# Hybrid decoder layer on one core: norm factors of three query projections moved into the exponentials, the first norm's row and the rotation tables moved later

## The chip, the cores and the metric

The kernel runs on one NeuronCore of a Trainium2 chip. The time of a run is the device time of that core in microseconds (us). The engines named below are TensorE (PE in the rows; its weight loads PEld), VectorE (DVE), ScalarE (ACT), GpSimd (POOL) and SyncE (SP), which here only issues DMAs. TensorE's clock has two levels, 1.2 and 2.4 GHz; a granted clock of 1.00 in a row is the higher one, 0.50 the lower.

## The reference

One decoder layer over 256 tokens of width 1024, all in float32. Cut to what matters here:

```python
hn = rmsnorm(h, mix_norm_g)                       # first norm
conv_a, conv_b, q, k_c, v_c, k_s, v_s, k_w, v_w, gate_logits = split(hn @ w_in)
y_conv = silu(layernorm(depthwise_conv31(conv_a * sigmoid(conv_b)) + b_dw))
y_nsa  = nsa_mixer(...)        # three softmax attentions on q: compressed keys (q as it is),
                               # selected blocks and window (q, k rotated by partial_rope(positions))
h = h + concat(y_conv, y_nsa) @ w_out
hq = rmsnorm(h, mem_q_norm_g)                     # second norm
h = h + memory_attention(hq, rmsnorm(mem, mem_kv_norm_g), ...)   # softmax(q k^T / 16) v @ w_o
hp = rmsnorm(h, peer_norm_g)                      # third norm
s  = (hp @ peer_w_q) . sub_keys                   # 8 heads x 2 sides x 128 scores per token
# top 16 of each side, top 16 of the 256 sums, gates = softmax over these 16
h = h + sum over experts of gates * gelu(hp . u_e) * v_e
return rmsnorm(h, final_norm_g)

def rmsnorm(x, g): return x * rsqrt(mean(x * x, -1) + 1e-6) * g
```

An RMS norm multiplies each token's vector by one number, 1/rms, after the gain. A projection is linear, so this number can be applied to the product instead. In a softmax over scores of one token the positive number can be applied as late as in the exponential: exp(r * (s - max s)).

## The kernel before

Activations lie transposed: 128 features on the partitions, the 256 tokens along the row. A projection takes the raw activations times the gain (hx for the first norm, g1 for the second, gx for the third) and makes one output chunk of 128 features by 256 tokens in PSUM. The first projection (`proj1`, L160) uses plain float32: 8 products, 16 matmul records of 128x256 per chunk. The later ones (`proj`, L156) split each operand into a high and a low part and take three products (24 matmuls per chunk); `wsplit` (L134) makes the parts of each 128x1024 weight chunk with two ScalarE copies (hi) and two subtractions (lo) on VectorE, or on GpSimd for the first 34 expert chunks. Weight chunks of 512 KB are loaded through SP's queue into four buffers `raw`.

The norm factor is made by the class `Rstd` (L197). `add` squares one chunk on ScalarE and adds it up on VectorE. `sums` (L214) takes the column sums with two tiny matmuls (ss), makes 1/rms on VectorE with twelve dependent instructions on 128x2 (m, sh, rsc, t) and two diagonal matrices dg. `rows` (L229) turns that into a 128x256 tile with the factor of every token along the row: two products with `ones` (sr), one ScalarE copy. `col` is the factor with tokens on the partitions, `row` the one with tokens along the row. The first norm (tag x) makes its row in the middle of chunk pa1, the second (tag h1) behind the third query chunk of the memory attention (L765 to L772), the third (tag h2) behind the third of 16 expert-query chunks (L846 to L861). (The rows print h1 and h2 without their numbers, as sr_h and dg_h.)

The stages in order: 14 warm-up matmuls; four pairs pb, pa of convolution chunks; two chunks kv; six chunks pq (two of keys, four of queries) with `rope` (L374: a permutation matmul rp, two multiplies with the tables Ct and St and an add on VectorE); the chunk group pv in natural layout; then 16 attention units of scores, softmax and transposes, interleaved by hand with the memory keys and values as filler matmuls (`fill`); w_out; the memory attention's queries (`mq_chunk`, `mq_out`, `m_scores`); w_mem_o; expert queries (`pq_out`, `key_scores`); then 128 expert chunks u and 128 v with the expert choice on VectorE behind the first.

The depthwise convolution is 124 VectorE instructions on yc (31 taps for 4 chunks, `tap`), handed out a few at a time by `conv(n)`; the rest must be done at unit 12, where `ln_mean` adds up the four chunks and TensorE's matmul pmu (L616) takes the mean over the channels.

TensorE's order is the program's. The order on VectorE, ScalarE, GpSimd and SP is made by a planner when the kernel is built: it takes the earliest instruction in program order that is ready by its own estimate of times, so it also takes later ones early into gaps. At run time each engine's queue is fixed and in order. PSUM has two tags of four slots: "mm" for projections, "at" for small and attention tiles.

The rotation tables: L250 and L251 load the positions to all 128 partitions (each reads the same 1 KB) between the first weight chunk and the rest of x; L263 to L279 make the angles on VectorE with two columns (`inv`, `sgn`) of the parameter tile `par`; L333 to L335 make St and Ct with ScalarE's Sin and load the Tanh table again.

Of the kernel before, what the change touches and what calls it, by code (L numbers as in the profile page):

```python
# [20 lines left out]
P = 128  # L21
T = 256
# [12 lines left out]
for _name, _w in (("mix_g", 8), ("memq_g", 8), ("memkv_g", 8), ("peer_g", 8), ("conv_w", 4 * TAPS),  # L35
                  ("conv_b", 4), ("ln_g", 4), ("ln_b", 4), ("cmp_b1", 2), ("cmp_b2k", 1),
                  ("cmp_b2v", 64), ("cmp_pos", 32), ("inv", 1), ("sgn", 1)):
    PC[_name] = (_n, _n + _w)
    _n += _w
# [12 lines left out]
def constants():  # L52
# [37 lines left out]
def rope_constants():  # L90

    d = np.arange(P) % 64
    inv = (np.float32(500000.0) ** (-(np.arange(8, dtype=np.float32) * np.float32(2.0) / np.float32(16.0)))).astype(np.float32)
    return np.stack([np.where(d < 16, inv[d % 8], 0.0), np.where(d < 8, -1.0, np.where(d < 16, 1.0, 0.0))], axis=1).astype(np.float32)


def build(tc, A, out, dbg=None):
# [99 lines left out]
    class Rstd:  # L197
# [16 lines left out]
        def sums(self):  # L214
# [9 lines left out]
            rsqrt(y, m, t, sh)  # L224
            self.diag = mwk.tile([P, 2, P], F32, name=f"dg_{self.tag}", tag="rs_d", bufs=1)
# [24 lines left out]
    posi = wk.tile([P, T], I32, name="posi", tag="rt")  # L250
    nc.sync.dma_start(posi, A["pos"].partition_broadcast(P))  # L251
# [9 lines left out]


    posf = wk.tile([P, T], F32, name="posf", tag="tb")  # L263
    V.tensor_copy(posf, posi)
    ang = St = ch.tile([P, T], F32, name="St")
    V.tensor_scalar(ang, posf, Pm("inv"), None, op0=ALU.mult)
    kk = wk.tile([P, T], F32, name="kk", tag="ta")
    MAGIC = 12582912.0
    V.tensor_scalar(kk, ang, 1.0 / (2.0 * math.pi), MAGIC, op0=ALU.mult, op1=ALU.add)
    V.tensor_scalar(kk, kk, MAGIC, None, op0=ALU.subtract)  # L270
    c1 = 6.28125
    c2 = float((np.array([2.0 * math.pi - c1], np.float32).view(np.uint32) & np.uint32(0xFFFFF000)).view(np.float32)[0])
    c3 = 2.0 * math.pi - c1 - c2
    for c in (c1, c2, c3):
        V.scalar_tensor_tensor(ang, kk, -c, ang, op0=ALU.mult, op1=ALU.add)
    PIF = 3.1415925
    V.tensor_scalar(ang, ang, PIF, -PIF, op0=ALU.min, op1=ALU.max)
    aabs = Ct = ch.tile([P, T], F32, name="Ct")
    V.scalar_tensor_tensor(aabs, ang, -1.0, ang, op0=ALU.mult, op1=ALU.max)  # L279
    halfpi = cst.tile([P, 1], F32, name="halfpi")  # L280
    V.memset(halfpi, math.pi / 2)
# [30 lines left out]
    for i in range(4):  # L312
        pb = psum(T, f"pb{i}")
# [7 lines left out]
        pa = psum(T, f"pa{i}")  # L321
        proj1(pa, wa, hx, range(4))
# [3 lines left out]
        proj1(pa, wa, hx, range(4, KC))  # L326
# [6 lines left out]
    S.activation(St, ang, AF.Sin, scale=Pm("sgn"))  # L333
    S.activation(Ct, aabs, AF.Sin, scale=-1.0, bias=halfpi)
# [53 lines left out]
    for i in range(6):  # L388
# [3 lines left out]
        V.tensor_mul(dst, ps, r0.row)  # L392
# [26 lines left out]
    V.tensor_scalar(chalf, r0.col, 0.5, None, op0=ALU.mult)  # L419
    for hf in range(2):  # L420
# [90 lines left out]
    def cmp_scores(hf):  # L511
# [12 lines left out]
        S.activation(sc, sc, AF.Exp, scale=0.125)  # L524
# [23 lines left out]
    def scores(c, g, hf):  # L548
# [174 lines left out]
    def mq_out(i, ps):  # L723
        t = twk.tile([P, T], F32, name=f"mqt{i}", tag="mqt", bufs=4)
        V.tensor_mul(t, ps, r1.row)
        S.activation(mq_h[:, i], t, AF.Copy)
        V.tensor_sub(mq_l[:, i], t, mq_h[:, i].bitcast(F32))

    def m_scores(h):
        for hf in range(2):  # L730
# [9 lines left out]
            V.tensor_scalar(mx, mx, -0.0625, None, op0=ALU.mult)  # L740
            sm = twk.tile([P, 1], F32, name=f"msm{h}{hf}", tag="msm", bufs=4)
            pe = mpe[h, hf] = twk.tile([P, T], F32, name=f"mpe{h}{hf}", tag="mpe", bufs=3)
            S.activation(pe, ps, AF.Exp, scale=0.0625, bias=mx, accum_out=sm)
# [79 lines left out]

    skp = tp.tile([P, 16, P], F32, name="skp")
# [285 lines left out]
def layout(inp):  # L1110
# [11 lines left out]
        np.broadcast_to(b2[1][None, :], (P, 64)), pos_l, rope_constants()], axis=1))  # L1122
# [48 lines left out]
```

## Time and profile before

| | |
|---|---|
| median of three runs | 1082.49 us (1081.40 to 1082.73) |
| profiled execution | 1082.72 us, its span 1080.9 us |
| busy, share of the span | TensorE 98%, VectorE 81%, ScalarE 54%, GpSimd 9% |
| chain of work that ended last | TensorE 85%, VectorE 13%, ScalarE 1%, DMA 1% |
| HBM read | 179.81 MB, 167 GB/s over the span |

Matmuls are pipelined and their ends are modelled, so the busy share of TensorE says little by itself; the distances between the starts of matmuls and the waits are to be read.

### The profile page before, as it was taken

Reading aid. Unit: us, or ns where it says so; the run is one execution under the profiler, and the core shown is the slowest. Engines: PE = TensorE matmul, PEld = TensorE weight load, DVE = VectorE, ACT = ScalarE, POOL = GpSimd, SP = SyncE. Lnnn points to the kernel's source line nnn. Section 1 sums busy time; section 2 is a strip of 40 time slices with the busy share of each in tenths; the row PEclk is TensorE's granted clock in tenths of the full one; section 3 lists DMA queues with packets and bytes.
Section 4 is the critical chain, followed back from the end, with each engine's and each line's share of the span. In section 5 each row is a group of like instructions: output and inputs, shape, how many; then the busy total and the mean of one; then the engine's idle time right before and its main releaser. Section 6 shows DMA issues by size and latency. Waiting matters only on the chain.

```text
span 1080.9 us, 20534 instructions
## 1 busy us (share of the span) xinstructions
PE 1061.2 (98%) x7346; PEld 976.3 (90%) x7346; DVE 871.8 (81%) x2226; ACT 580.0 (54%) x1334; POOL 102.3 (9%) x82
## 2 busy tenths in 40 slices
PE   8999999999999999999999999999999999999997
PEld 7889878999999999999999999998888888888885
DVE  4998888978889998889999999986666666666665
ACT  4224676566455555665555555455555555555554
POOL 0000000000039992000000000001000000000000
PEclk9999999999999999999999999999999999999999
DMA  7744333525435555444554444466555555555552
GB/s 245 247 127 151 98 99 117 196 98 174 159 116 178 178 193 167 160 162 157 162 164 163 163 150 160 156 203 201 194 190 193 194 192 192 195 194 193 195 195 78
DMA packets 51685, 182.45 MB, mean 169 GB/s; under 512 B 5760, under 2 KB 6528, under 8 KB 51456
## 3 DMA queue, kind: packets, MB, share of 16 engines
q1 hardware_dynamic: 51296, 180.62, 50.8%
q8 instruction: 58, 0.95, 0.4%
q10 hardware_dynamic: 288, 0.52, 0.1%
q14 instruction: 43, 0.35, 0.1%
HBM read 179.81 MB, written 1.05 MB: 167 GB/s over the span
## 4 chain that ended last, share of the span: by engine, by line
PE 85%; DVE 13%; ACT 1%; DMA 1%; issue 0%; SPq 0%; DVEq 0%; ACTq 0%
PE Y L1071 32%; PE pu L152 9%; PE pu L154 8%; PE pu L153 8%; PE pq L163 2%; PE pw L1017 1%; PE ppq L152 1%; PE ppq L153 1%; PE ppq L154 1%; PE pb L163 1%; PE pw L1018 1%; PE pa L163 1%; DVE ohx L948 1%; PE pmk L152 1%; DVE lo L142 1%; DVE ohx L946 1%
## 5 line engine op out<-in xcount | busy, mean ns | idle before, releaser
L141 ACT ACTIVATE hi<-raw 128x512 fp32r<-128x512 f32 x624 | 376.7, 626 | 176.7 <-PE pu L153 66.9
L142 DVE TENSOR_TENSOR lo<-raw,hi 128x512 fp32r<-128x512 f32 x556 | 369.1, 687 | 26.8 <-ACT hi L141 21.0
L152 PE MATMUL pu<-hn_h,hi 128*128 128x256 f32 x1024 | 296.3, 289 | 0.0
L154 PE MATMUL pu<-hn_h,lo 128*128 128x256 f32 x1024 | 290.7, 284 | 1.9 <-DVE lo L142 1.9
L153 PE MATMUL pu<-hn_l,hi 128*128 128x256 f32 x1024 | 290.7, 284 | 0.0
L154 PEld LDWEIGHTS pu<-hn_h,lo 128*128 128x128 f32 x1024 | 197.3, 193 | 2.1 <-DVE lo L142 2.1
L153 PEld LDWEIGHTS pu<-hn_l,hi 128*128 128x128 f32 x1024 | 197.4, 193 | 0.0
L152 PEld LDWEIGHTS pu<-hn_h,hi 128*128 128x128 f32 x1024 | 197.2, 193 | 0.0
L1071 PE MATMUL Y<-hi,al 128*128 128x512 f32 x512 | 158.3, 389 | 0.0
L1071 PE MATMUL Y<-lo,ah 128*128 128x512 f32 x512 | 158.3, 389 | 0.0
L1071 PE MATMUL Y<-hi,ah 128*128 128x512 f32 x512 | 158.2, 389 | 0.0
L1071 PEld LDWEIGHTS Y<-hi,al 128*128 128x128 f32 x512 | 96.1, 188 | 20.0
L1071 PEld LDWEIGHTS Y<-lo,ah 128*128 128x128 f32 x512 | 96.1, 188 | 19.9
L1071 PEld LDWEIGHTS Y<-hi,ah 128*128 128x128 f32 x512 | 96.1, 188 | 19.8
L167 DVE TENSOR_TENSOR al<-slB,ah 128x256 fp32r<-128x256 f32 x88 | 37.4, 425 | 86.1 <-PE Y L1071 86.1
L166 ACT ACTIVATE ah<-slB 128x256 fp32r<-128x256 f32 x88 | 36.8, 418 | 110.7 <-PE Y L1071 110.7
L142 POOL TENSOR_TENSOR lo<-raw,hi 128x512 fp32r<-128x512 f32 x68 | 94.8, 1421 | 11.8 <-ACT hi L141 9.2
L1023 ACT ACTIVATE slB<-pw 128x348 f32<-128x348 f32 (+31 forms) x64 | 32.5, 507 | 70.2 <-DVE slB L1022 57.0
L298 DVE SCALAR_TENSOR_TENSOR yc<-u,par,yc 128x256 f32<-128x256 f32 x120 | 54.8, 474 | 0.1
L167 DVE TENSOR_TENSOR al<-slA,ah 128x256 fp32r<-128x256 f32 x40 | 17.1, 428 | 37.3 <-PE Y L1071 37.3
L166 ACT ACTIVATE ah<-slA 128x256 fp32r<-128x256 f32 x40 | 16.7, 418 | 49.3 <-PE Y L1071 48.0
L152 PE MATMUL ppq<-gx_h,hi 128*128 128x256 f32 x128 | 37.4, 292 | 0.0
(372 smaller groups left out, 1745.7 us busy)
## 6 DMA issues: line engine op xcount, KB each, us to landing
raw<-u SPq DMA_DIRECT2D x128, 512.0 KB, 3.4
raw<-v SPq DMA_DIRECT2D x128, 512.0 KB, 3.3
raw<-peer_w_q SPq DMA_DIRECT2D x16, 512.0 KB, 3.3
raw<-w_in_t SPq DMA_DIRECT2D x15, 512.0 KB, 3.8
raw<-w_mem_k SPq DMA_DIRECT2D x8, 512.0 KB, 4.5
raw<-w_mem_v SPq DMA_DIRECT2D x8, 512.0 KB, 3.3
raw<-w_out SPq DMA_DIRECT2D x8, 512.0 KB, 3.4
raw<-w_mem_q SPq DMA_DIRECT2D x8, 512.0 KB, 3.5
```

Of the source, the lines that this page charges most:

```text
L141: S.activation(hi, r, AF.Copy)
L142: (engs or (V, V))[q].tensor_sub(lo, r, hi.bitcast(F32))
L152: PE.matmul(ps, w[0], xh, start=start, stop=False)
L153: PE.matmul(ps, w[0], xl, start=False, stop=False)
L154: PE.matmul(ps, w[1], xh, start=False, stop=stop)
L163: PE.matmul(ps, w[0][:, k * P:(k + 1) * P], x[:, k], start=k == 0, stop=k == KC - 1)
L166: S.activation(dst[0], src, AF.Copy)
L167: V.tensor_sub(dst[1], src, dst[0].bitcast(F32))
L298: V.scalar_tensor_tensor(yc[:, i], u[:, i, j:j + T], w, yc[:, i], op0=ALU.mult, op1=ALU.add)
L946: V.tensor_tensor(o4, o4, tif[:, side].unsqueeze(2).to_broadcast([P, 16, 16, 8]), op=ALU.mult)
L1023: S.activation(slB[:, done - J:, n0:n0 + 4].rearrange("p i n -> p n i"), pw[:, :, done:], AF.Copy, scale=1.0 / GSC)
L1071: PE.matmul(Y[nh][c], lhs[:, sl], wc[c][t], start=False, stop=i == KEYS - 1 and lhs is a[1], skip_group_check=True)
```

## The change

For the queries of three attentions the norm factor is no longer multiplied into the projected tile; the tile is copied as it is, and the factor of the token, which stands on the partitions in the scores, goes as a column into the exponential's scale and into the negated maximum. The second norm therefore makes no row. The third still does, one chunk later, because the expert inputs hn need it. The first norm's row moves from the middle of pa1 to its end, and pb0 and pa0, which wait for it, take "at" slots of PSUM. The load of the positions and the angle instructions move behind the four pairs of convolution chunks, into separate buffers; `inv` and `sgn` move from `par` to the second part of the constants, which is loaded there. The key scores of each expert-query chunk run one chunk later than the chunk instead of two.

```diff
     w0 = wload(A["w_in_t"][0])
-    posi = wk.tile([P, T], I32, name="posi", tag="rt")
-    nc.sync.dma_start(posi, A["pos"].partition_broadcast(P))
     for q in range(1, 4):
         nc.sync.dma_start(xT[:, 2 * q:2 * q + 2], A["xT"][:, 2 * q:2 * q + 2])
...
-        pb = psum(T, f"pb{i}")
+        pb = psum(T, f"pb{i}", "mm" if i else "at")
...
-        proj1(pa, wa, hx, range(4))
+        proj1(pa, wa, hx)
         if i == 1:
             r0.rows()
             conv_in(*pend)
-        proj1(pa, wa, hx, range(4, KC))
...
     nc.sync.dma_start(con2, A["con"][:, NCON1:])
+    posi = wk.tile([P, T], I32, name="posi", tag="rt")
+    nc.sync.dma_start(posi, A["pos"].partition_broadcast(P))
+    Ct = ch.tile([P, T], F32, name="Ct")
+    St = ch.tile([P, T], F32, name="St")
     posf = wk.tile([P, T], F32, name="posf", tag="tb")
     V.tensor_copy(posf, posi)
-    ang = St = ch.tile([P, T], F32, name="St")
-    V.tensor_scalar(ang, posf, Pm("inv"), None, op0=ALU.mult)
+    ang = wk.tile([P, T], F32, name="ang", tag="th")
+    V.tensor_scalar(ang, posf, C("inv"), None, op0=ALU.mult)
...
-    S.activation(St, ang, AF.Sin, scale=Pm("sgn"))
-    S.activation(Ct, aabs, AF.Sin, scale=-1.0, bias=halfpi)
+    S.activation(St, ang, AF.Sin, scale=C("sgn"))
+    V.scalar_tensor_tensor(kk, ang, -1.0, ang, op0=ALU.mult, op1=ALU.max)
+    S.activation(Ct, kk, AF.Sin, scale=-1.0, bias=halfpi)
...
-        V.tensor_mul(dst, ps, r0.row)
+        if i < 2:
+            V.tensor_mul(dst, ps, r0.row)
+        else:
+            S.activation(dst, ps, AF.Copy)
...
+    r8, r8n = [ch.tile([P, 2], F32, name=f"r8{j}") for j in range(2)]
+    V.tensor_scalar(r8, r0.col, 0.125, None, op0=ALU.mult)
+    V.tensor_scalar(r8n, r0.col, -0.125, None, op0=ALU.mult)
...
-        S.activation(sc, sc, AF.Exp, scale=0.125)
+        S.activation(sc, sc, AF.Exp, scale=r8[:, hf:hf + 1])
...
-        V.tensor_scalar(mx, mx, -0.125, None, op0=ALU.mult)
+        V.tensor_scalar(mx, mx, r8n[:, hf:hf + 1], None, op0=ALU.mult)
...
-            S.activation(pe[:, b, 0:W], ps[:, b], AF.Exp, scale=0.125, bias=mx[:, b:b + 1], accum_out=sm[:, b:b + 1])
+            S.activation(pe[:, b, 0:W], ps[:, b], AF.Exp, scale=r8[:, hf:hf + 1], bias=mx[:, b:b + 1], accum_out=sm[:, b:b + 1])
...
     def mq_out(i, ps):
-        t = twk.tile([P, T], F32, name=f"mqt{i}", tag="mqt", bufs=4)
-        V.tensor_mul(t, ps, r1.row)
-        S.activation(mq_h[:, i], t, AF.Copy)
-        V.tensor_sub(mq_l[:, i], t, mq_h[:, i].bitcast(F32))
+        split((mq_h[:, i], mq_l[:, i]), ps)
...
-    pq0 = mq_chunk(0)
-    r1.sums()
-    pq1 = mq_chunk(1)
-    pq2 = mq_chunk(2)
-    r1.rows()
-    mq_out(0, pq0)
-    mq_out(1, pq1)
-    mq_out(2, pq2)
-    for i in range(3, KC):
+    r16 = [mp.tile([P, 2], F32, name=f"r16{j}") for j in range(2)]
+    for i in range(KC):
         mq_out(i, mq_chunk(i))
+        if i == 1:
+            r1.sums(rows=False)
+            for j in range(2):
+                V.tensor_scalar(r16[j], r1.col, (0.0625, -0.0625)[j], None, op0=ALU.mult)
...
-        V.tensor_mul(qt, ps, r2.row)
+        S.activation(qt, ps, AF.Copy)
...
-        todo.append((i, ps))
-        if i == 0:
+        todo.append((i, pq_out(i, ps)))
+        if i == 1:
             r2.sums()
-        if i < 2:
-            continue
-        if i == 2:
+            V.tensor_copy(r2c, r2.col)
+        if i == 3:
             r2.rows()
-            todo = [(j, pq_out(j, p)) for j, p in todo]
-            continue
-        todo[-1] = (i, pq_out(i, ps))
-        key_scores(*todo.pop(0))
-        if i == 3:
+        if i:
             key_scores(*todo.pop(0))
...
-            tc.keep_in_program_order(S.activation(ge, ge, AF.Exp))
+            tc.keep_in_program_order(S.activation(ge, ge, AF.Exp, scale=r2c[:, hf:hf + 1]))
```

With `rows=False`, `sums` returns before it makes the two diagonals. In the memory attention's scores the maximum is multiplied by `r16[1]` and the exponential scaled by `r16[0]` in the same way as above.

## Rows read from the trace of the kernel before

**Rows 1.** Waits of TensorE, whole span: engine, line, releaser: us, times, longest.
```profile
PE sr_c L233 <- DVE dg_c L227: 2.3, 1, 2.3
PE pb L163 <- DVE hx L259: 2.1, 1, 2.1
PE pu L154 <- DVE lo L142: 1.9, 1, 1.9
PE sr_h L233 <- DVE dg_h L227: 1.4, 1, 1.4
PE pmu L616 <- DVE asm L565: 1.1, 1, 1.1
...
PE sr_x L233 <- DVE dg_x L227: 0.9, 1, 0.9
```
**Rows 2.** Chain of waits, 0 to 30 us: start us, us, what.
```profile
2.57 6.08 DMA posi<-pos
...
10.00 4.53 PE pb L163 x12
14.53 3.45 PE pa L163 x16
...
21.44 0.35 PE ss_x L218 x4
...
24.51 0.71 PE sr_x L233 x4
```
**Rows 3.** Stages: from:to us, length, busy us (instructions) per engine, clock, DMA share, GB/s.
```profile
6.00:7.00 1.00, 1.00 (x8) 1.00 (x8) 0.00 (x0) 0.00 (x0) 0.00 (x0) 1.00 0.85 144
...
9.00:10.00 1.00, 0.00 (x0) 0.00 (x1) 0.96 (x4) 0.43 (x2) 0.00 (x0) 1.00 1.05 412
...
26.00:75.00 49.00, 49.00 (x231) 43.01 (x230) 48.88 (x144) 9.67 (x24) 0.00 (x0) 1.00 0.59 186
75.00:150.00 75.00, 75.00 (x563) 66.24 (x563) 64.92 (x202) 46.22 (x140) 0.00 (x0) 1.00 0.37 121
...
420.00:423.00 3.00, 3.00 (x16) 3.00 (x16) 2.93 (x8) 0.63 (x1) 0.00 (x0) 0.50 0.51 175
```
**Rows 4.** Line 129 (second half of w0, issued at 2.10 us): time to landing.
```profile
DMA to landing us min/median/max: 4.0/4.0/4.0
```
**Rows 5.** Line 253 (three later pieces of x, first issued 3.05): time to landing.
```profile
DMA to landing us min/median/max: 6.5/6.7/6.9
```
**Rows 6.** Timeline of VectorE, 7 to 16 us: start, us, line, operation, idle before.
```profile
8.67 0.29 DVE L264 CAST posf<-posi 128x256 f32<-128x256 int32 x1 [3.35 <-DMA posi<-pos]
...
10.46 0.35 DVE L259 TENSOR_SCALAR hx<-xT,par 128x256 f32<-128x256 f32 x1
...
11.06 0.35 DVE L259 TENSOR_SCALAR hx<-xT,par 128x256 f32<-128x256 f32 x1
...
15.09 0.43 DVE L279 SCALAR_TENSOR_TENSOR Ct<-St 128x256 f32<-128x256 f32 x1
```
**Rows 7.** Timeline of all engines, 0 to 14 us: pb's first matmuls.
```profile
6.90 1.03 PE L163 MATMUL pb<-hx,raw 128*128 128x256 f32 x4
```
**Rows 8.** VectorE by line and shape, 26 to 320 us: count, busy, mean ns, idle.
```profile
L392 DVE TENSOR_TENSOR qraw<-pq,rs_x 128x256 f32<-128x256 f32 x4 | 1.7, 416 | 0.0
```
**Rows 9.** Timeline of all engines, 14 to 45 us: ScalarE's second table load.
```profile
16.48 1.28 ACT L335 ACT_TABLE_LOAD   x1
...
17.77 0.20 ACT L335 ACTIVATE halfpi<-Ct 128x1 f32<-128x1 f32 x1
```
**Rows 10.** Timeline of TensorE, 204 to 209 us, around the second norm's row.
```profile
205.75 0.28 PE L153 MATMUL pmq<-g_l,hi 128*128 128x256 f32 x1
205.87 0.28 PE L154 MATMUL pmq<-g_h,lo 128*128 128x256 f32 x1
...
207.97 0.36 PE L152 MATMUL pmq<-g_h,hi 128*128 128x256 f32 x1
```
**Rows 11.** Timeline of all engines, 312 to 314.6 us: end of the expert queries.
```profile
312.33 0.63 ACT L141 ACTIVATE hi<-raw 128x512 fp32r<-128x512 f32 x1 [0.81 <-PE ppq L153]
312.45 0.43 DVE L831 TENSOR_TENSOR pqt<-ppq,rs_h 128x256 f32<-128x256 f32 x1 [0.22 <-PE ppq L154]
```

More of the change, by code (lines that the diff above doesn't have):

```diff
@@ L36 @@
                   ("conv_b", 4), ("ln_g", 4), ("ln_b", 4), ("cmp_b1", 2), ("cmp_b2k", 1),
-                  ("cmp_b2v", 64), ("cmp_pos", 32), ("inv", 1), ("sgn", 1)):
+                  ("cmp_b2v", 64), ("cmp_pos", 32)):
     PC[_name] = (_n, _n + _w)
@@ L85, in constants @@
     put("rsel", rs.reshape(P, 512))
+    inv = (np.float32(500000.0) ** (-(np.arange(8, dtype=np.float32) * np.float32(2.0) / np.float32(16.0)))).astype(np.float32)
+    put("inv", np.where(d < 16, inv[d % 8], 0.0)[:, None])
+    put("sgn", np.where(d < 8, -1.0, np.where(d < 16, 1.0, 0.0))[:, None])
     put("iota16", np.broadcast_to(cc[None, :], (P, 16)))
     return c
[L90 to L94, printed above, removed]
 def build(tc, A, out, dbg=None):
@@ L212, in add, with sums @@
             self.k += 1
-        def sums(self):
+        def sums(self, rows=True):
             ps = psum(2, f"ss_{self.tag}", "at")
@@ L224, in sums @@
             rsqrt(y, m, t, sh)
+            if not rows:
+                return
             self.diag = mwk.tile([P, 2, P], F32, name=f"dg_{self.tag}", tag="rs_d", bufs=1)
@@ L260, in build @@
         r0.add(xT[:, k])
-    posf = wk.tile([P, T], F32, name="posf", tag="tb")
-    V.tensor_copy(posf, posi)
-    ang = St = ch.tile([P, T], F32, name="St")
-    V.tensor_scalar(ang, posf, Pm("inv"), None, op0=ALU.mult)
[L267 to L281, printed above, removed]
     u = ch.tile([P, 4, 30 + T], F32, name="u")
@@ L320, in build @@
             nc.sync.dma_start(con1, A["con"][:, 0:NCON1])
-        pa = psum(T, f"pa{i}")
-        proj1(pa, wa, hx, range(4))
+        pa = psum(T, f"pa{i}", "mm" if i else "at")
+        proj1(pa, wa, hx)
         if i == 1:
@@ L332, in build @@
     nc.sync.dma_start(con2, A["con"][:, NCON1:])
-    S.activation(St, ang, AF.Sin, scale=Pm("sgn"))
-    S.activation(Ct, aabs, AF.Sin, scale=-1.0, bias=halfpi)
+    posi = wk.tile([P, T], I32, name="posi", tag="rt")
+    nc.sync.dma_start(posi, A["pos"].partition_broadcast(P))
+    Ct = ch.tile([P, T], F32, name="Ct")
+    St = ch.tile([P, T], F32, name="St")
+    posf = wk.tile([P, T], F32, name="posf", tag="tb")
+    V.tensor_copy(posf, posi)
+    ang = wk.tile([P, T], F32, name="ang", tag="th")
+    V.tensor_scalar(ang, posf, C("inv"), None, op0=ALU.mult)
+    kk = wk.tile([P, T], F32, name="kk", tag="ta")
+    MAGIC = 12582912.0
+    V.tensor_scalar(kk, ang, 1.0 / (2.0 * math.pi), MAGIC, op0=ALU.mult, op1=ALU.add)
+    V.tensor_scalar(kk, kk, MAGIC, None, op0=ALU.subtract)
+    c1 = 6.28125
+    c2 = float((np.array([2.0 * math.pi - c1], np.float32).view(np.uint32) & np.uint32(0xFFFFF000)).view(np.float32)[0])
+    c3 = 2.0 * math.pi - c1 - c2
+    for c in (c1, c2, c3):
+        V.scalar_tensor_tensor(ang, kk, -c, ang, op0=ALU.mult, op1=ALU.add)
+    PIF = 3.1415925
+    V.tensor_scalar(ang, ang, PIF, -PIF, op0=ALU.min, op1=ALU.max)
+    halfpi = cst.tile([P, 1], F32, name="halfpi")
+    V.memset(halfpi, math.pi / 2)
+    S.activation(St, ang, AF.Sin, scale=C("sgn"))
+    V.scalar_tensor_tensor(kk, ang, -1.0, ang, op0=ALU.mult, op1=ALU.max)
+    S.activation(Ct, kk, AF.Sin, scale=-1.0, bias=halfpi)
     S.activation(halfpi, Ct[:, 0:1], AF.Tanh)
@@ L739, in m_scores @@
             V.tensor_reduce(mx, ps, axis=AX.X, op=ALU.max)
-            V.tensor_scalar(mx, mx, -0.0625, None, op0=ALU.mult)
+            V.tensor_scalar(mx, mx, r16[1][:, hf:hf + 1], None, op0=ALU.mult)
             sm = twk.tile([P, 1], F32, name=f"msm{h}{hf}", tag="msm", bufs=4)
             pe = mpe[h, hf] = twk.tile([P, T], F32, name=f"mpe{h}{hf}", tag="mpe", bufs=3)
-            S.activation(pe, ps, AF.Exp, scale=0.0625, bias=mx, accum_out=sm)
+            S.activation(pe, ps, AF.Exp, scale=r16[0][:, hf:hf + 1], bias=mx, accum_out=sm)
             V.reciprocal(sm, sm)
@@ L821, in build @@
     show("h2", h2T)
+    r2c = tk.tile([P, 2], F32, name="r2c")
     skp = tp.tile([P, 16, P], F32, name="skp")
@@ L1121, in layout @@
         a["cmp_b1"][0].T, np.concatenate([b2[0], b2[0]])[:, None],
-        np.broadcast_to(b2[1][None, :], (P, 64)), pos_l, rope_constants()], axis=1))
+        np.broadcast_to(b2[1][None, :], (P, 64)), pos_l], axis=1))
     o["pos"] = a["positions"][0]
```

2 lines of the change are left out of this document (1 added, 1 removed).

## The prediction

> **What bounds the kernel now.** I read four views in this order. The list of what TensorE waited for [rows 1] comes first: over the whole span there are, behind the start-up, only six waits of 0.9 us or more, 9.7 us together, so this kernel is paced by TensorE's matmuls, and an edit gains only where it shortens one of these waits, takes matmuls away or keeps the clock up. The reader should note which three the diff touches: the one before pb (2.1), before sr_h (1.4) and before sr_x (0.9); two others hang on VectorE's queue (pmu 1.1, sr_c 2.3), which the diff reloads. The chain of waits over the first 30 us [rows 2] then shows where the 2.1 us come from: it runs through the load of the positions, 6.08 us from issue, to angle instructions that stand in front of hx on VectorE. It shows a second loss too: 12 matmuls of pb take 4.53 us, where the next 16 of the same shape take 3.45. The stages [rows 3] tell how full VectorE is: 48.88 of 49 us between 26 and 75, 64.92 of 75 between 75 and 150. Last, the timelines at each edit.
>
> **Start: positions and tables moved away.** The second half of w0 lands at 2.10 + 4.0 = 6.1 [rows 4]; the next piece of x, issued at 3.05, only at 3.05 + 6.5 = 9.55 [rows 5]. Between them the queue carries positions (128 KB, the same kilobyte read for every partition), and the rate falls to 144 GB/s in 6 to 7 us, against 412 in 9 to 10 [rows 3]. Without it x's second piece (262 KB) lands at 6.1 + 0.64 = 6.8 by the better rate, at 7.9 by the worse; I take 7.0, nearer the better, because the slow stretch is the one in which positions move. One hx of 0.35 us later [rows 6] TensorE can go on at about 7.4; its first four matmuls, from 6.90, keep it until 7.9 [rows 7]. So the wait goes, and with it the slow 12 matmuls: at 3.45/16 = 0.216 they take 2.59 instead of 4.53. The whole first group would end at 6.9 + 3.45 = 10.4, plus its pipelined start, instead of 14.53: 4.0 us at most. What is late next is VectorE's own pace: hx follows hx every 0.60 us, at 10.46 and 11.06 [rows 6], TensorE wants one every 0.43; over the six remaining that costs up to 1.0, less the 0.5 of lead. And w1, which must land by 10.4, follows two more pieces of x. I take 3.7. Bounds: if the positions only cost their bytes (131 KB at 412 GB/s = 0.3) the gain is 0.35; the other end is 4.0. On SP's queue the loads behind posi issue one slot earlier. Posi itself now stands behind con2, where SP waits for a free weight buffer; whom it slows there (weights of pa2, mT) has a lead of up to four chunk buffers, and the tables are first read by rope, two stages on.
>
> **First norm's row later.** Its two column-sum steps stay; sr_x moves from the middle of pa1 to its end. From the end of ss_x at 21.8 to sr_x at 24.51 [rows 2] the small chain takes 2.7 us; a whole pa1 (3.45) now covers it. The 0.9 us wait goes, with 0.7 us to spare; that is its gain, bounded by nothing and 0.9 (if mT lands earlier and its splits slip in between the small instructions). The price: the convolution's inputs, and all that VectorE does after them, start half a chunk (1.73 us) later against TensorE. pb0 and pa0 wait in the other PSUM tag, whose four slots hold them, warm and ss_x; nothing queues for them.
>
> **Angles behind the convolution.** Nine VectorE instructions, from posf to Ct (the first and the last in [rows 6]; 3.2 us together), leave a stretch where VectorE idled and enter one where it is 99.8% busy [rows 3]. Leaving it are four qraw multiplies of 0.416 [rows 8], now ScalarE copies. Net 1.55 us, with the 1.73 above 3.3 us by which VectorE is behind TensorE. Convolution taps are fillers, not due until the channel sum in front of pmu, and VectorE has 75 - 64.92 = 10.1 us free between 75 and 150. But its queue is in order, and TensorE already waits 1.1 us at pmu: taps pushed behind the last free moment reach TensorE one for one. Bounds 0 and 3.3; I take half, 1.5 us lost, since the free time is three times the delay but is spread in pieces. Behind that wait stand all later scores and fillers on TensorE.
>
> The angles also move Sin behind the convolution's Tanh. A table load took 1.28 us here, with the next ACTIVATE directly behind it [rows 9]; there are two for Sin and back as before, perhaps one more before the first Tanh. ScalarE is busy 9.67 of 49 us in that stretch [rows 3], so I count nothing; at worst the first Tanh starts 1.28 later, which adds to the 3.3. The Trainium skill ("ScalarE: Activation LUTs", What ACT_TABLE_LOAD costs) speaks against such moves more loudly: 2.66 us for each switch, a load of 1.283 and a drain of 1.38. By it the extra one would cost 2.66 instead of 1.28 and the sum come out an estimated 1.4 us worse at most; the trace has the load at 1.28 and no such drain behind it.
>
> **Second norm without a row.** In the query projection of the memory attention the last matmul before sr_h starts at 205.87, the first behind at 207.97; its neighbours follow each other every 0.12 [rows 10]. So the four sr_h and the 1.4 us wait cost 2.10 - 0.12 = 1.98 us, and all of it goes: six buffers of low halves let VectorE split two chunks ahead, and nothing else waits there. Eight multiplies (3.4 us), two diagonals and a ScalarE copy leave as well, off the path. Lower bound of the gain: the four matmuls alone, about 0.5, if a weight split is late instead.
>
> **Third norm and key scores.** The 16 multiplies become ScalarE copies; TensorE sees one of them. After the last projection there used to be 12 psq matmuls to cover the last pqt (0.43 us from 312.45); now four stand there (0.44), and the copy may queue behind a weight split of 0.63 on ScalarE from 312.33 [rows 11]. TensorE then idles 0.1 to 1.0 before the last key scores, and the last sco, the expert choice on VectorE and Y start as much later. I take 0.5 lost. The choice itself, which ends in the 1.9 us wait at pu [rows 1], keeps its work, so that wait stays.
>
> **Scales as columns.** 44 exponentials read a column for their scale, and the small maxima multiply by one. No row shows what it adds; between nothing and a whole pass over such a tile (0.42 each as in [rows 8], 18 us) it fits in ScalarE's 75 - 46.22 = 28.8 us of idle time [rows 3]. Nothing.
>
> **Sum.** -3.7 - 0.9 - 2.0 + 0.5 + 1.5 = -4.6 us. The profiled execution took 1082.72 (its span 1080.9); it becomes 1078.1. The median of the runs shown is 1082.49, 0.23 lower, so 1077.9.
>
> **Rivals.** (a) *The load, not the positions.* x's second piece is late because early loads are slow; w0, too, needs 4.0 us to land [rows 4]. Against it: the rate doubles as soon as posi has landed. Start gain 0.35, the clock still falls: -0.35 - 0.9 - 2.0 + 0.5 + 1.5 = -1.25, so 1081.2. (b) *The channel sum takes it back.* All 3.3 us arrive at pmu, the wait becomes 4.4, and the clock falls, as it did after the 1.9 us wait at pu (0.50 in 420 to 423 [rows 3]); I price that as at the start, 4.53 - 2.59 = 1.9. For it: a full VectorE; against: its 10.1 free us. -6.6 + 0.5 + 5.2 = -0.9, so 1081.6. (c) *Slower: the taps pile up.* VectorE's order is planned anew. If the planner lets angles, kv and rope go first and the taps lose the lead that fills 26 to 75 now, up to the 10.1 us that are free after 75 are to be worked off in one piece in front of pmu, where TensorE waits 1.1 already; with the clock's 1.9 that is 12 against a gain of 6.1: 1088. It decides from an added wait of about 4.2 us. Against it: each free piece takes taps, as 1.1 us at pmu shows for now. (d) *More than forecast.* VectorE's 3.4 us less in the memory attention and an earlier mT remove pmu's 1.1 and nothing is lost at the sum: -3.9 - 0.9 - 2.0 + 0.2 - 1.1 = -7.7, so 1074.8.
>
> **Numbers.** Forecast 0.52 (1076 to 1080), (a) 0.14, (b) 0.13, (c) 0.09, (d) 0.12. About 0.2%, 2.2 us, is what a measurement here tells from no change: faster is below 1080.3. Forecast and (d) lie below it but for some 0.02, and of (a) and (b) a third does: 0.62 + 0.09 = 0.71. Same are the rest of these, 0.02 + 0.18 = 0.20. Slower is (c), 0.09. Range 1074.5 to 1081.8: it holds forecast, (d) and most of (a) and (b), and leaves out (c) and the tails.
>
> **What would show it.** No wait of pb above 0.5 us and a granted clock of 1.00 from 10 to 14 us; pa beginning near 10.5. No wait at sr_x. No sr between the memory attention's projections, the matmuls 0.12 apart through there. A wait at the last psq below 1 us. The wait at pmu: 1 to 4.5 us, the number that I know least; above 5 it makes the forecast wrong, as does x's second piece landing after 8.5.

## Result: slower by 1.1%, and the largest part of it in a stage that the change does not touch

The changed kernel takes 1093.3 us (median of 4 runs, 1091.45 to 1094.92) against 1081.95 (1080.44 to 1082.73) for the kernel before in the same comparison: ratio 1.0106, 95% interval 1.0086 to 1.0126. The forecast was 1077.9. The profiled execution of the changed kernel took 1094.92 us, its span is 1093.1 (before: 1082.72 and 1080.9).

The waits of TensorE over the whole span (as in [rows 1]: engine, line, releaser: us, times, longest):

```profile
PE pmu L620 <- DVE lsum L614: 4.6, 1, 4.6
PE pu L150 <- DVE lo L138: 2.6, 1, 2.6
PE sr_c L231 <- DVE dg_c L225: 2.4, 1, 2.4
PE pb L159 <- DVE hx L255: 1.5, 2, 1.3
...
PE psq L840 <- ACT pqt L831: 0.4, 1, 0.4
```

The waits at sr_x and sr_h are gone, the one at pb is shorter. But pmu's has grown from 1.1 to 4.6 us, pu's from 1.9 to 2.6. Together these make the list 2 us longer, no explanation for 11. So the next view is where TensorE stands: the start of the same group of matmuls in both traces, after minus before.

| group | starts before | starts after | after minus before |
|---|---|---|---|
| first pa | 14.4 | 11.9 | -2.5 |
| pkv | 40.6 | 36.9 | -3.7 |
| pmu (channel sum) | 152.6 | 152.9 | +0.3 |
| ss_c, first matmuls after the low clock | 162.8 | 165.3 | +2.5 |
| pmq, memory queries | 196.3 | 200.0 | +3.6 |
| pms, behind the second norm | 213.8 | 215.3 | +1.5 |
| pu | 318.6 | 320.2 | +1.7 |
| end of pu | 725.0 | 727.0 | +2.0 |
| end of the v stage | 1073.2 | 1085.4 | +12.2 |

The rows up to pmq hold some scatter: from ss_c to w_out (pwo) the traces of six kernels whose instructions up to there are those of before take 7.6 us twice and 8.9 to 9.2 four times; the changed kernel took 8.6. Up to the v stage the change has lost 2 us; in the v stage, 128 chunks of unchanged code, it loses 10 more. Two stretches of the kernel before, at the start and inside that stage (columns as in [rows 3]: us, busy us and instructions of PE, PEld, DVE, ACT and POOL, clock, DMA share, GB/s):

```profile
10.00:14.00 4.00, 4.00 (x11) 3.30 (x12) 4.00 (x15) 3.16 (x6) 0.00 (x0) 0.57 0.87 349
...
730.00:1050.00 320.00, 320.00 (x1414) 265.07 (x1413) 202.08 (x354) 172.56 (x354) 2.59 (x1) 1.00 0.59 194
```

and stretches of the kernel after:

```profile
6.00:7.00 1.00, 0.90 (x5) 0.45 (x3) 0.00 (x0) 0.00 (x0) 0.00 (x0) 1.00 0.87 217
9.00:10.00 1.00, 0.79 (x4) 0.30 (x2) 0.86 (x3) 0.55 (x2) 0.00 (x0) 1.00 1.04 402
10.00:14.00 4.00, 4.00 (x18) 2.97 (x17) 2.19 (x8) 1.11 (x3) 0.00 (x0) 1.00 0.83 298
26.00:75.00 49.00, 49.00 (x230) 42.71 (x229) 47.66 (x142) 16.02 (x38) 0.00 (x0) 1.00 0.59 194
75.00:150.00 75.00, 72.54 (x558) 63.99 (x556) 67.21 (x209) 49.22 (x144) 0.00 (x0) 1.00 0.32 106
...
145.00:153.00 8.00, 3.36 (x25) 2.74 (x25) 7.66 (x23) 3.98 (x13) 0.00 (x0) 0.89 0.28 77
153.00:157.00 4.00, 4.00 (x16) 3.13 (x16) 3.75 (x12) 1.69 (x5) 0.00 (x0) 0.50 0.66 240
730.00:1050.00 320.00, 320.00 (x1374) 257.70 (x1373) 197.61 (x344) 167.44 (x344) 3.06 (x1) 1.00 0.60 189
```

In the same 320 us TensorE gets through 1,374 matmuls instead of 1,414. It is busy all the time in both, at a granted clock of 1.00 in both, with nearly the same DMA share, and VectorE and ScalarE have room in both. The distances between the starts of the stage's 1,536 matmuls say it exactly: 226.7 ns in the mean before, all but four of them 225 to 228; 233.3 after, for the most part alternately 235 to 236 and 231 to 232. ("Pace" below is this mean distance.) That is 1,536 x 6.6 ns = 10.2 us. A busy share of 100% hides it; counting instructions in a stretch of fixed length shows it.

The chain of waits at the start, after (as in [rows 2]: start us, us, what):

```profile
3.05 6.07 DMA xT<-xT
9.12 0.03 issue
9.14 0.36 DVE hx L255
9.51 0.04 issue
9.55 2.49 PE pb L159 x8
12.04 3.45 PE pa L159 x16
```

No angle instruction stands in it any more, the granted clock from 10 to 14 us is 1.00 instead of 0.57, and the first pa begins at 12.04 instead of 14.53.

### The profile page after: what moved, and what is told of

It reads as the page before. It is cut to its first block, busy times and chain, and to the rows that moved or that the text cites. A ratio compares the mean times of both kernels' runs of the same rounds, so it can differ in the third digit from the quotient of the medians.

```text
span 1093.1 us, 20529 instructions
## 1 busy us (share of the span) xinstructions
PE 1071.1 (98%) x7342; PEld 975.0 (89%) x7342; DVE 863.9 (79%) x2201; ACT 586.9 (54%) x1353; POOL 101.7 (9%) x82
## 4 chain that ended last, share of the span: by engine, by line
PE 81%; DVE 15%; DMA 1%; ACT 1%; issue 1%; SPq 0%; DVEq 0%; ACTq 0%
PE Y L1066 32%; PE pu L148 9%; PE pu L150 8%; PE pu L149 8%; DVE yc L273 2%; PE pw L1012 1%; PE ppq L149 1%; PE ppq L148 1%; PE ppq L150 1%; PE pw L1013 1%; DVE ohx L943 1%; PE pmk L148 1%; PE pmv L457 1%; PE pmk L150 1%; PE pmw L149 1%; PE pmv L459 1%
## 5 line engine op out<-in xcount | busy, mean ns | idle before, releaser
L138 DVE TENSOR_TENSOR lo<-raw,hi 128x512 fp32r<-128x512 f32 x556 | 369.4, 687 | 31.5 <-ACT hi L137 28.1
L1066 PE MATMUL Y<-lo,ah 128*128 128x512 f32 x512 | 161.8, 396 | 0.0
L1066 PE MATMUL Y<-hi,ah 128*128 128x512 f32 x512 | 161.8, 396 | 0.0
L1066 PE MATMUL Y<-hi,al 128*128 128x512 f32 x512 | 161.8, 396 | 0.0
```

The lines of the kernel that those rows point to most:

```text
L138: (engs or (V, V))[q].tensor_sub(lo, r, hi.bitcast(F32))
L1066: PE.matmul(Y[nh][c], lhs[:, sl], wc[c][t], start=False, stop=i == KEYS - 1 and lhs is a[1], skip_group_check=True)
```

## Experiments

The theories after the result: A, the new tile r2c (8 bytes, placed as 32) moves every tile behind it in its pool's side by 32 bytes, among them the tiles ah and al of the v stage, and their address sets the pace (they are its stationary tiles: of a matmul's two inputs the one that is loaded beforehand, PEld in the rows; the other one, here hi and lo, is the moving tile); B, something dynamic does (order, DMA, clock). C, the angle instructions on a full VectorE make the wait at pmu; D, the later row does. The experiments ran on three chips, each against the kernel before on its own chip (medians 1082.7 to 1083.3 there).

**1. The tile wider (e1_row128).** On the changed kernel:

```diff
-    r2c = tk.tile([P, 2], F32, name="r2c")
+    r2c = tk.tile([P, 32], F32, name="r2c")[:, 0:2]
```

> The changed kernel with one difference: the new tile r2c is 128 bytes per partition wide instead of 32, of which 8 are used. Nothing is computed otherwise. In the change its 32 bytes moved slA and the stationary tiles ah and al of the v stage from addresses that are 32 modulo 64 to 0 modulo 64; with 128 bytes they are at 32 modulo 64 again, as in the kernel before, and the instructions are the same. Theory A (the address of the stationary tiles sets the pace of the v stage): the 1,536 matmuls of the stage start 226.7 ns apart again instead of 233.3, time 1093.3 - 10.2 = about 1083.1 us. Rival B (the pace comes from what runs beside the stage or ran before it: order of the instructions, DMA, clock): 233 ns, about 1093 us.

Measured 1091.81 us, ratio to before 1.0084 (1.0071 to 1.0098). In the stretch of the v stage:

```profile
730.00:1050.00 320.00, 320.00 (x1379) 259.43 (x1378) 198.46 (x345) 168.00 (x345) 2.78 (x1) 1.00 0.59 189
```

Neither theory as it stood: the pace is not back, yet the mean is another one (232.4 ns) and so is the pattern, which now repeats every seven matmuls (228, 230, 233, 241, 232, 231, 232). Only the width of a tile differs from the changed kernel, so an address matters; "32 modulo 64" was the wrong form of it.

**2. The kernel before with 32 bytes more (e2_pad32).**

```diff
+    pad = tk.tile([P, 2], F32, name="pad")
+    G.memset(pad, 0.0)
```

> The kernel before with one difference: a tile of 32 bytes per partition, set to zero once and never read, in the pool in which the change puts r2c. Its instructions are otherwise those of before; slA, ah and al move by 32 bytes as in the change. Theory A (address): the v stage slows from 226.7 to 233.3 ns a matmul, 1082.0 + 10.2 = about 1092 us. Rival B (what runs beside or ran before): 226.7 ns, about 1082 us.

1090.97 us, ratio 1.0067 (1.0052 to 1.0083):

```profile
730.00:1050.00 320.00, 320.00 (x1373) 257.60 (x1372) 196.64 (x343) 166.82 (x343) 2.77 (x1) 1.00 0.58 189
```

The v stage takes on the changed kernel's pace and pattern (233.3; 235 and 231 to 232) without any part of the change. B falls: 32 bytes that nobody reads cost 7.7 us (5.6 to 9.0 by the interval). That is less than the 10.2 of the stage, and the padding gives back only about 0.5 elsewhere (the chunks pmw, whose matmuls start 117 instead of 120 ns apart, take 30.3 instead of 30.8 us up to the expert queries). The profiled execution, 1093.52, was the slowest of the four. Where the rest is, no run shows.

**3. Many places in one run (e3_map).**

```diff
-            hi = wts.tile([P, 512], F32R, ...)
+            hi = wts.tile([P, 520], F32R, ...)    # lo likewise
...
+        o = 8 * (i % 4)
-        ah = tmp.tile([P, T], F32R, name=f"ah{i}", tag="ah")
+        ah = tmp.tile([P, T + 32], F32R, name=f"ah{i}", tag="ah")[:, o:o + T]    # al likewise
```

> The kernel before with the operands of the v stage at many addresses in one run: the stationary tiles ah, al lie at 0, 32, 64 or 96 bytes behind their usual place by the number of the chunk modulo 4, and the buffers of hi and lo are 2080 bytes apart instead of 2048, so that the moving operands too lie at 0, 32, 64 and 96 modulo 128. Theory A: the distance between starts changes from chunk to chunk with the address of the stationary tile, 226.7 ns at odd multiples of 32 and 233.3 at even ones (or with the place of stationary against moving). Rival B: one distance for all chunks.

1087.11 us in one run. The distances lie between 224 and 240 ns. Their means by the stationary tile's place modulo 128 (231.3 to 232.8) are no better sorted than by the moving one's (231.0 to 232.5); by pairs of both they run from 230.6 to 234.6. With the places changing at every chunk no steady pattern forms. It refutes "one distance for all" and the simple form of A, and no more. What it suggested was to keep a place for some chunks, and to look at the distance between the two operands: in the kernel before, ah and hi are a multiple of 512 bytes apart.

**4. A scan of the distance (e5_scan).** On the kernel before:

```diff
+        o = 8 * (i // 8)
-        ah = tmp.tile([P, T], F32R, name=f"ah{i}", tag="ah")
+        ah = tmp.tile([P, T + 128], F32R, name=f"ah{i}", tag="ah")[:, o:o + T]    # al likewise
```

> The kernel before, with the stationary tiles ah and al of the v stage moved by 32 bytes every eight chunks: 16 places, 0 to 480 bytes, one after the other; hi and lo stay. Theory A2 (what counts is the distance from the stationary to the moving tile modulo 512 bytes, which is 0 in the kernel before, 32 in the change, 128 in the first experiment): the mean distance between starts is 226.7 ns in the first block of 96 matmuls, 233.3 in the second (with a pattern of 235 and 231 ns), 232.4 in the fifth (with a pattern that repeats every seven matmuls). Rival A1 (the place of the stationary tile modulo 64): 226.7 in every second block. Rival B: one distance in all blocks.

Mean distance between starts in each block of 96 matmuls, without its first 12, from the start times in the trace:

| ah minus hi, modulo 256 bytes | 0 | 32 | 64 | 96 | 128 | 160 | 192 | 224 |
|---|---|---|---|---|---|---|---|---|
| first eight blocks, ns | 226.8 | 233.3 | 233.3 | 234.2 | 232.4 | 233.4 | 228.9 | 233.2 |
| second eight blocks, ns | 226.8 | 233.3 | 233.3 | 234.2 | 232.4 | 233.4 | 228.9 | 233.3 |

The time was 1091.13 us in one run. Five stretches of 20 us lie, but for 1 us at most, in the blocks with ah moved by 0, 32, 128, 192 and 256 bytes:

```profile
727.00:747.00 20.00, 20.00 (x90) 16.54 (x89) 12.07 (x22) 10.53 (x22) 2.77 (x1) 1.00 0.62 207
749.00:769.00 20.00, 20.00 (x88) 16.09 (x87) 12.04 (x21) 10.26 (x21) 0.00 (x0) 1.00 0.55 184
816.00:836.00 20.00, 20.00 (x88) 16.22 (x87) 12.29 (x22) 10.23 (x21) 0.00 (x0) 1.00 0.58 186
858.00:878.00 20.00, 20.00 (x89) 16.37 (x88) 12.19 (x22) 10.29 (x22) 0.00 (x0) 1.00 0.61 189
903.00:923.00 20.00, 20.00 (x90) 16.57 (x89) 12.39 (x22) 11.11 (x24) 0.00 (x0) 1.00 0.57 187
```

The three values foretold are there, with their patterns, in one execution at one clock. The table repeats after 256 bytes, not only after the 512 that I had assumed. Of eight places seven cost 2.1 to 7.4 ns a matmul. The table holds for a stream that keeps one distance: in experiment 3, where it changes from matmul to matmul, the matmuls at distance 0 took 231.0 ns in the mean, and all eight classes lie between 230.8 and 233.3.

**5. Distance or address (e6_all32).** On the kernel before, ahead of everything on that side:

```diff
     con1 = cst.tile([P, NCON1], F32, name="con1")
+    pad = cst.tile([P, 2], F32, name="pad")
+    G.memset(pad, 0.0)
```

> The kernel before with a tile of 32 bytes per partition, set to zero and never read, ahead of all tiles of the left side, so that raw, hi, lo, hn, ah, al and slA all move by 32 bytes together. Theory A2 (distance between stationary and moving tile): the v stage stays at 226.7 ns, about 1083 us. Rival A1 (the stationary tile's own address): ah and al are where the change has them, 233.3 ns, about 1092 us.

1082.35 us, ratio 0.9997 (0.9983 to 1.0011), pace 226.7 ns:

```profile
730.00:1050.00 320.00, 320.00 (x1414) 265.05 (x1413) 202.35 (x354) 172.61 (x354) 0.71 (x1) 1.00 0.58 193
```

ah and al lie exactly where the change has them, and the stage is fast, because hi and lo moved along. It is the distance, not the place of the stationary tile alone.

**6. The change with the distance restored (e7_row512).** As in experiment 1, with `[P, 128]`.

> The changed kernel with r2c 512 bytes per partition wide (8 used), so that ah and al stand a multiple of 512 bytes from hi and lo again. Theory A2: 226.7 ns a matmul in the v stage and 1093.3 - 10.2 = about 1083.1 us: no gain and no loss against the kernel before, because the wait at pmu and the low clock behind it take the start's gain back. Rivals A1, B: about 1092 us.

1084.64 us (12 runs), ratio 1.0020 (1.0005 to 1.0035):

```profile
730.00:1050.00 320.00, 320.00 (x1414) 265.05 (x1413) 202.90 (x354) 171.94 (x353) 2.77 (x1) 1.00 0.59 195
```

The v stage is back at its old pace, and by the two ratios 9.3 us are gone. What is left of the change is its edits' own work, and that is a small loss, not a gain.

**7. Tables early, behind x (e4_early).** On the kernel of experiment 1:

```diff
         if i == 0:
             nc.sync.dma_start(con1, A["con"][:, 0:NCON1])
+            posi = wk.tile([P, T], I32, name="posi", tag="rt")
+            nc.sync.dma_start(posi, A["pos"].partition_broadcast(P))
+            ...    # the nine angle instructions, inv and sgn from par
...
-    nc.sync.dma_start(posi, A["pos"].partition_broadcast(P))
-    ...    # the nine angle instructions
```

The table iota16 in the constants is zero in this kernel, so the numbers of the chosen experts are others; no instruction differs by it.

> The kernel of the first experiment (r2c 128 bytes wide) with the positions loaded behind x, the second weight chunk and the first constants instead of behind the convolution chunks, and the angle instructions directly behind chunk pa0; inv and sgn stand in par as in the kernel before. Theory C (the twelve angle instructions on a full VectorE are what makes TensorE wait 4.6 us for the channel sum at pmu, and the clock fall behind it): the wait falls to about 1 us, no stretch at 0.50 follows, and the time is 1083.1 - 3.5 = about 1079.6 us. Rival D (the delay of VectorE comes from the later row of the first norm, or the early load costs the start as much as it gives): pmu waits over 3 us still, or the start falls back, about 1082 to 1083 us.

1083.63 us (11 runs) against 1091.81 for the kernel of experiment 1: -8.2 us, more than twice what C gave. (Both theories had reckoned from 1083.1 us, a time that experiment 1 did not reach, so the drop is to be compared and not the time.) TensorE's wait at pmu is 0.7 us, and ScalarE ends it:

```profile
PE pmu L621 <- ACT ape L569: 0.7, 1, 0.7
```

**8. Both repaired (e8_early512).** Tables early and r2c 512 bytes wide, iota16 in place:

> The kernel with r2c 512 bytes wide as above and the positions and angles early but behind x, as in the experiment that brought the time from 1091.8 to 1083.6 us. The two causes lie in different stages, so their prices should add: 1083.6 - 8.6 (1,536 matmuls from 232.4 to 226.7 ns, 8.8) = about 1074.9 us, below both kernels; if they do not add (rival: the later stages give part of it back), 1077 us or more.

1077.37 us (6 runs), ratio 0.9944 (0.9924 to 0.9963): faster than both kernels. Against e7, on the same chip, the early tables bring 7.3 us; the distance brings 6.7 by the ratios of e4 and e8, which ran on different chips, where the two prices had promised 1074.9 us. Of the 2.5 us that are missing the traces show 1.6 between the channel sum and pwo: in 163 to 168 us the clock is lower in the profiled execution of e8,

```profile
163.00:168.00 5.00, 4.48 (x25) 4.51 (x26) 2.83 (x10) 1.89 (x6) 0.00 (x0) 0.66 0.22 86
```

than in that of e4,

```profile
163.00:168.00 5.00, 4.54 (x39) 4.57 (x40) 3.88 (x13) 3.13 (x10) 0.00 (x0) 1.00 0.23 88
```

and pwo starts 3.0 us earlier than in the kernel before where in e4 it starts 4.7 earlier. Why the clock fell in one and not in the other, no run tells. It need not be a property of e8: this is the stretch from ss_c to pwo that takes 7.6 or 8.9 to 9.2 us with the instructions of before (with early tables 7.1 in e4, e9 and e10, 8.5 to 8.6 in e8 and e11). The traces therefore do not settle whether the two prices add. The distance is worth less in the medians wherever it can be compared: by the ratios 6.7 and 6.9 us (e4 and e8, e1 and e7) where the paces give 8.8, and 7.7 (experiment 2) and 9.3 (change and e7) where they give 10.2. Where C's 7 us are is seen on VectorE. First e7 (start us, us, line, operation, idle before):

```profile
18.06 0.23 DVE L546 CAST causb<-con 128x128 bf16<-128x128 f32 x1 [5.20 <-DMA con<-con]
...
36.14 0.29 DVE L314 CAST posf<-posi 128x256 f32<-128x256 int32 x1
36.34 0.49 DVE L273 SCALAR_TENSOR_TENSOR yc<-u,par,yc 128x256 f32<-128x256 f32 x1
36.73 0.35 DVE L316 TENSOR_SCALAR ang<-posf,con 128x256 f32<-128x256 f32 x1
...
152.43 0.42 DVE L614 TENSOR_TENSOR lsum<-lsum,lsum 128x256 f32<-128x256 f32 x1
```

then e8:

```profile
12.33 0.28 DVE L305 CAST posf<-posi 128x256 f32<-128x256 int32 x1
...
15.40 0.43 DVE L321 SCALAR_TENSOR_TENSOR Ct<-St 128x256 f32<-128x256 f32 x1
19.45 0.16 DVE L220 TENSOR_SCALAR m_x<-ss_x 128x2 f32<-128x2 f32 x1 [3.63 <-PE ss_x L218]
...
148.02 0.42 DVE L616 TENSOR_TENSOR lsum<-lsum,lsum 128x256 f32<-128x256 f32 x1
```

Early, the angles fill 12.3 to 15.8 us, where VectorE has nothing else to do; late, VectorE idles there for 5.2 us, and the angles come later, between taps. The last sum before pmu comes 4.4 us earlier with early tables. The rest of the 7 is TensorE's clock: in the changed kernel it stands still from 148 to 152.93 and then runs slowly:

```profile
147.69 0.60 PE L585 MATMUL ptt<-con,ape 128*128 128x128 f32 x4
152.93 1.19 PE L620 MATMUL pmu<-lsum,ones 128*128 128x256 f32 x2 [4.64 <-DVE lsum L614]
154.05 0.58 PE L557 MATMUL pss<-k_h,q_h 64*128 64x256 f32 x1
...
155.93 0.41 PE L457 MATMUL pmv<-hi,mg 128*128 128x256 f32 x1
156.15 0.41 PE L458 MATMUL pmv<-lo,mg 128*128 128x256 f32 x1
```

pmv every 0.21 to 0.22 us instead of 0.12, clock 0.50 in 153 to 157 (shown above). In e8 it is 1.00 there:

```profile
153.00:157.00 4.00, 4.00 (x30) 2.98 (x28) 3.19 (x9) 2.78 (x10) 0.00 (x0) 1.00 0.36 125
```

**9. The distance in the u stage (e9_u32, e10_u64).** On e8, with 8 and 16 for n:

```diff
     h2p = outer.enter_context(tc.tile_pool(name="h2p", bufs=1))
+    pad = h2p.tile([P, n], F32, name="pad")
+    G.memset(pad[:, 0:2], 0.0)
...
-    r2c = tk.tile([P, 128], F32, name="r2c")[:, 0:2]
+    r2c = tk.tile([P, 128 - n], F32, name="r2c")[:, 0:2]
```

> The 1077.4 us kernel (tables early behind x, r2c 512 bytes wide) with 32 bytes of padding ahead of hx, gx and hn and 32 bytes less in r2c: the v stage keeps its distance of 0 modulo 512 between stationary and moving tile, but in the expert queries and the u stage the moving tiles gx and hn now stand 32 bytes off the stationary hi and lo instead of 0. With distance 0 the 3,004 matmuls of the u stage start 120.0 ns apart (median, kernel before); in the chunks pmw the distance is 0 in the kernel before (120.0 ns) and 480 in the change and in the kernel with the padding of 32 bytes (117.0 ns). Theory A3 (the distance acts on every split projection, and 0 is a bad place for 256 columns): u at 117 to 118 ns, 3,456 matmuls times 2 to 2.5 ns = 7 to 8.6 us less, 1069 to 1070.5 us. Rival E (the u stage waits for the parts of the weights, not for the matmuls): no change, 1077.4 us.

> As the kernel with 32 bytes ahead of hx, gx and hn, with 64 bytes: the distance in the expert queries and the u stage is 448 modulo 512 instead of 480. Theory A3: also below 120 ns, about 118 by the mixed places of the run with displaced buffers (448: median 118.0, 168 matmuls), 1070 us. Rival E: 1077.4 us.

1074.30 us (5 runs), ratio 0.9915 (0.9902 to 0.9929), and 1073.46 (4 runs), 0.9908 (0.9892 to 0.9924): the fastest kernels of this study, not to be told apart. The distances in the u stage fell as A3 said, from 120.0 to 117 and 118 ns (medians), but the gain is 3 to 4 us and not 7 to 8.6. Nor is all of that the distance: in the trace of e9 1.2 us of 3.1 are there when pwo starts (the clock, which stays at 1.00 in 163 to 168 us), 0.8 come in the expert queries and 0.8 in the u stage. Sums as small as these are no firmer than the scatter: the u stage lasts 405.0 us in the trace of e8 and 404.2 in that of e9, but 404.2 in that of e4 too, where the u stage has the distance of e8. In e9 the wait at the expert choice eats most of what the matmuls gain; e8 has 2.3 us there, e9:

```profile
PE pu L154 <- DVE lo L142: 6.1, 1, 6.1
```

and a stretch ahead of it, e8 and then e9:

```profile
340.00:410.00 70.00, 70.00 (x585) 70.00 (x585) 69.80 (x224) 38.75 (x75) 64.65 (x46) 1.00 0.55 182
```

```profile
340.00:410.00 70.00, 67.55 (x580) 67.35 (x578) 69.76 (x223) 40.74 (x78) 60.58 (x45) 1.00 0.54 174
```

VectorE is busy 69.8 of 70 us in both: the choice sets the end of this part, and faster matmuls only wait longer for it. Rival E holds up to the end of the choice: what TensorE waits for there is lo, a part of the weights, which VectorE makes behind the choice. A3 holds before and behind it by the paces, but what it brings there is of the size of the scatter.

**10. The first norm's row (e11_rowmid).** On e8, the row back in the middle of pa1:

```diff
-        proj1(pa, wa, hx)
+        proj1(pa, wa, hx, range(4))
         if i == 1:
             r0.rows()
             conv_in(*pend)
+        proj1(pa, wa, hx, range(4, KC))
```

> The 1077.4 us kernel with the first norm's row made in the middle of chunk pa1 again, as in the kernel before. By the prediction's term (the wait at sr_x, 0.9) TensorE waits 0.9 us at sr_x again and everything behind comes 0.9 us later up to the channel sum: 1078.3 us. Rival (the row's place is worth nothing, because VectorE sets the end of the convolution): 1077.4 us, the wait is there but pmu starts at the same time.

1078.41 us (4 runs), ratio 0.9956 (0.9939 to 0.9972), not told apart from e8. The wait is back:

```profile
PE sr_x L235 <- DVE dg_x L229: 1.0, 1, 1.0
```

All groups from pkv on start 0.9 us later than in e8, and pmu starts at the same time (148.6 in both). The rival was right about that place, in the kernel with early tables: up to pmu VectorE sets the time. The medians, 1.3 us apart by the ratios and on different chips, do not decide between the two.

**11. The second norm alone (e12_second).** On the kernel before, only `mq_out`, the two scales in `m_scores` and the loop of the chunks as in the change.

> The kernel before with the second norm's part of the change alone: no row for the memory queries, the factor as a column in scale and maximum. No tile of the v stage moves. By the prediction's term: the waits at sr_h for the second norm and the four sr matmuls go, -2.0 us, about 1080.7 us against 1082.7. Rival (the copies that ScalarE makes from PSUM make the queries late, or the wait comes back at the memory scores): 1082.7 us.

1080.35 us (11 runs), ratio 0.9973 (0.9963 to 0.9983), 2.9 us less, with 1.8 to 4.0 inside the interval. In its trace pms starts 0.2 us earlier than in the kernel before where pwo, ahead of the edit, starts 2.0 later: 2.2. The prediction's 2.0 stands for that place. Behind it 0.7 us go again: pmw to the first expert queries takes 31.5 us instead of 30.8, as in e7.

## Why the prediction was wrong

**The step that failed first** is the one called "Scales as columns", which came out at "Nothing". It priced what the column costs the instructions that read it, and that was right as far as it went: the exponentials of the memory attention take 90 ns more each, on an engine with room. Before and after (ScalarE by line and shape, 200 to 240 us: count, busy, mean ns, idle):

```profile
L743 ACT ACTIVATE mpe<-pms,mmx 128x256 f32<-128x256 f32 x8 | 3.8, 472 | 4.2 <-DVE mmx L740 4.1
...
L744 ACT ACTIVATE mpe<-pms,mmx,r 128x256 f32<-128x256 f32 x8 | 4.5, 562 | 3.1 <-DVE mmx L741 2.9 <-PE pmt L753 0.2
```

It did not ask where the column lies. Its 32 bytes moved ah and al against hi and lo, and cost 10.2 us by the traced pace (7.7 to 9.3 by medians) in a stage that no part of the sum and no rival mentions: experiments 2 (the same pace without the change), 4, 5 and 6 (no loss with the distance restored) show it. The opening claim, that an edit gains or loses only by a wait, a number of matmuls or the clock, lacked this fourth way: the distance between matmuls of one shape is not a constant. Rival (c) foretold a slower kernel, but by taps that pile up at pmu, with an added wait of 4.2 us or more; the added wait was 3.5.

**The step mis-sized** is "Angles behind the convolution": +1.5 (0 to 3.3) for the wait at pmu. In e7, where nothing else disturbs, pmu starts 3.5 us later against its own start-up gain (from -3.1 to +0.4), takes 0.5 longer and leaves 2.3 more to the low clock: 6.3. "The free time is three times the delay" counted an average of free time over 75 us. In the changed kernel VectorE is still idle for 7.8 us between 75 and 150 (67.21 busy, shown above), and TensorE waits 4.6 at pmu all the same: the free time was not where the taps could take it. The row's half chunk, which I charged at 1.73, cost nothing where the angles stand early (experiment 10), and with the angles early the wait is gone though the row stays late (experiments 7 and 8); the row alone beside late angles was not run. Rival (b) had the mechanism, with a wait of 4.4 (measured 4.6) and the clock at 1.9 (measured 2.3 in e7, less in e1), and I gave it 0.13. The extra table load that was thought possible did not come: the start has three loads in both kernels.

**The start**: -3.7 and -0.9. In e1, e4, e7 and e8 pkv starts 3.1 to 3.5 us earlier than before, in the changed kernel 3.7, where 4.6 was forecast. The row's 0.9 is confirmed (experiment 10), which leaves 2.2 to 2.8 for the positions. But "before" is one trace. In the six traces whose start is that of the kernel before, pkv starts at 40.6, 40.6, 40.9, 41.2, 38.8 and 39.0; in the last two (e6, e3) the granted clock is 1.00 from 10 to 14 us in spite of the early positions. So about 2 us of the gain hang on whether the clock falls there, and the row and the positions together gave some 3.0 on average, 1.2 to 4.3 from trace to trace. The mechanism held: rate in 6 to 7 us 217 GB/s instead of 144 [rows 3], clock 1.00, no angle ahead of hx. Mis-sized was what is late next: TensorE still waits 1.5 us for hx (0.6 in e1, 1.8 in e7), because x's pieces land later than I took; the one on the chain lands at 9.12. And a start-up gain is worth what it brings to pmu, which the sum did not ask for.

**The second norm**: -2.0, measured at pms -2.1 in the change and -2.2 alone; some 0.7 are lost again in the memory attention. **Third norm and key scores**: +0.5; the wait at psq is 0.4, and the old one at Y's first matmuls (0.5) went with it, so nothing remains. **The expert choice's wait** "stays": it was 0.7 longer, 2.6, but kernels that keep the third norm as it was have 1.9 (before), 2.3 (e2) and 2.6 (e12), so this growth is not shown to be the change's.

Added up for e7, from group to group: -3.1 + 6.3 - 0.6 (pwo) - 2.1 + 0.7 (memory attention) + 0.1 + 0.7 (pu) = +2.0, its profile 1.9. Such a list adds up for any two traces; it places the time and proves no term, and terms below about 1 us are within the scatter.

## What to carry to other kernels

When a small tile is added, compare the addresses of all matmul operands before and after, and count the matmuls in a fixed stretch of every stage, touched or not; the busy share shows nothing. Price an instruction that is moved by what the engine does at either place in the order of its queue, not by the mean free time of a stretch: here 3.2 us of work, moved from an idle gap into the full run-up to a sum, became 7.3 in the medians (e7 and e8). A gain ahead of a stage that another engine paces is kept only if that engine gains as well.

## What the runs showed of the hardware

The distance between starts of 128x512 matmuls in fp32r, each with its own weight load (fp32r is the type of the high and low parts), depends, as long as the stream keeps one distance, on the distance in bytes between the stationary and the moving tile, modulo 256: 226.8 ns at 0, 228.9 at 192, 232.4 to 234.2 at the six other multiples of 32, with patterns that repeat after two (32), three (192) or seven matmuls (128), at a granted clock of 1.00. Moving both tiles together by 32 bytes changes nothing (experiment 6). With 256 columns the order is another: 120.0 ns at 0, 117 and 118 at 224 and 192 (the distances 480 and 448 of experiment 9). The Trainium skill (TensorE: Matmul & The Clock Gate, "Step-by-step: what each phase is for") gives the streaming operand and the weight load a read port each, so that loading weights takes nothing from a running matmul. That gives no reason for a pace that depends on the distance of the two; the scan has up to 7.4 ns a matmul by address alone, and the measurement decides. Whether the two reads share something, and what, no run here shows: a tile was always moved together with the instructions that write it.
